# Scales of q and k made during av, seven PSUM banks in turn, two stages' first loads moved forward, a subtraction on POOL

## The chip, the cores and the metric

The kernel runs on one core of a Trainium2 chip. The metric is the device time of one execution in microseconds. Engines are named as in the profile: PE (matmuls), PEld (PE's weight loads), DVE (VectorE), ACT (ScalarE), POOL (GpSimd), SP (which issues the DMAs). The granted clock is the share of TensorE's full clock that the throttle let through.

## The reference

One layer of a decoder trunk on 2048 tokens of width 1024, in float32. Cut to what matters:

```python
h = rmsnorm(x, g_norm)
a_u, a_v, a_gate, q, k, v, b_gate, gate_logits = split(h @ w_in)     # widths 1024, the last 2 x 1024
y_a = spatial_gating(gelu(a_u), gelu(a_v), w_s, b_s, g_v) * silu(a_gate)
y_b = dilated_attention(q, k, v) * silu(b_gate)      # 16 heads of 64; (128,1), (512,4), (2048,16)
g_a, g_b = split(sigmoid(gate_logits))
x = x + (g_a * (y_a @ w_proj_a) + g_b * (y_b @ w_proj_b)) @ w_out
return rmsnorm(x, g_final)
```

`spatial_gating` normalizes gelu(a_v) per token, mixes the 128 positions of each chunk with a masked 128x128 matrix per group of 128 channels, adds b_s and multiplies by gelu(a_u).

## The kernel before

Every float32 product is made of three: each factor is split in a high and a low part in the matmul's own 32-bit format (fp32r), and `mm3` (L97) accumulates hi·hi, hi·lo and lo·hi in PSUM. A weight arrives as `wraw` by one DMA; `ring` puts its two parts into a ring of eight buffers (names `wc`, `wch`, `wcl`; a trailing number in the listings is the buffer's serial number). `split_w` (L82) makes the high part on ACT (L83) and the low part, raw − hi, on DVE or POOL (L86): from av on, POOL does it.

The tokens are worked in two halves of 1024, and each half as two pieces of 512 columns (`X[0]`, `X[1]`, normalized and transposed input, split in two). Stages of a half, with the columns of w_in they use:

- v (5120): `unit_rows` L310, 16 PSUM tiles of 48 matmuls 128x256; the evacuation `ev_v` L347 writes `vst` (two halves in f16) with ACT L356 and DVE L357, and stores it to `v_d`. In the first half each of the four 256-column blocks also gets a scale (`wscale` L223).
- `make_T` L173: differences T1, T2, T3 of the input blocks for a seven-product scheme, each split on ACT (L134) and DVE (L135).
- av (1024): `unit_rows` again, gelu to `avr`, stored to `av_d`; then `make_T4` L189.
- k (4096) and q (3072): `unit_S` L236, four blocks m of 256 columns; each takes one 1 MB load (`wraw2`, two buffers), seven weight combinations W, and seven products of 12 matmuls 128x512, combined with DVE additions into four results. In the first half each block first calls `wscale` twice: a reduce over the columns' absolute values (DVE L227), a maximum over the partitions with that of g_norm (POOL L230, `partition_all_reduce`), and three small DVE operations. The scale keeps q and k within f16; `scales` L365 derives products of them for the attention.
- u and g (0 and 2048): `branch_a` L390 with two `unit_S`; for a group of 128 channels it loads `avg` (gelu(a_v)), the mixing matrix `wst` and `bsb`, and the evacuation of u multiplies by the mixing product `px` (L418).
- First half: b_gate and the first gate (6144, 7168). Between the halves: the second gate, `unit_P` L299.

Then `restore` rebuilds X[1], and the window (L651) runs the attention of 16 heads with filling matmuls between, `seg` by `seg`; `load_qk` and `load_v` fetch its data. The last stage merges and normalizes.

PSUM has eight banks: `pj` two, `pt` three, `ss` two (attention scores), `po` one. Outside the attention `unit_rows` and `unit_P` take `pj` alone, and `unit_S` `pj` and `pt` alternately.

The order on each engine is set when the program is built: a scheduler places instructions by priority and estimated cost, and each engine then runs its own list strictly in that order. A DMA stands in SP's list and waits there for its data and its buffer; what stands behind it waits too.

Of the kernel before, what the change touches and what calls it, by code (L numbers as in the profile page):

```python
# [16 lines left out]
P = 128  # L17
# [10 lines left out]
class Prog:  # L28
    def __init__(self, ctx, tc, io):
        self.ctx, self.tc, self.nc, self.io = ctx, tc, tc.nc, io  # L30
        self.last_pe = None
        self.w_hi, self.w_lo = self.nc.scalar, self.nc.vector
        self.x_lo = self.nc.vector


    def setup(self):
        nc, tc, ctx, io = self.nc, self.tc, self.ctx, self.io
        self.const = c = ctx.enter_context(tc.tile_pool(name="const", bufs=1))
        self.ps = ctx.enter_context(tc.tile_pool(name="ps", bufs=1, space=bass.MemoryType.PSUM))
        dr = ctx.enter_context(tc.tile_pool(name="dr", bufs=1, space=bass.MemoryType.DRAM))  # L40
        self.xp = ctx.enter_context(tc.tile_pool(name="xp", bufs=1))
        self.wk = ctx.enter_context(tc.tile_pool(name="wk", bufs=2))
        self.gn = c.tile([P, KC], F32, name="gn")
        nc.scalar.dma_start(out=self.gn, in_=io["g_norm"])
# [9 lines left out]
        self.sq = c.tile([P, 8], F32, name="sq")  # L54
        self.sk = c.tile([P, 8], F32, name="sk")
# [67 lines left out]
    def pt(self):  # L123
        return self.ps.tile([P, 512], F32, name="pt", tag="pt", bufs=3)


    def alloc_X(self, tt):
        return [[self.xp.tile([P, 512], F32R, name=f"X{tt}_{k}_{p}", tag=f"X{tt}_{k}_{p}") for p in range(2)]
# [44 lines left out]
    def make_T(self, hp, qds):  # L173

        nc = self.nc
        self.TT = {}
        for i in (1, 2, 3):
            self.TT[i] = [[self.tp.tile([P, 512], F32R, name=f"T{i}_{k}_{p}", tag=f"T{i}_{k}_{p}") for p in range(2)]
                          for k in range(4)]
        for k in range(4):  # L180
            b12, b11, b22 = (self.h_chunk(hp, "ht", 4, qds[c], k + r) for c, r in ((1, 0), (0, 0), (1, 4)))
            nc.vector.tensor_sub(b11, b12, b11)
            self.split_X(self.TT[1], k, b11)
            nc.vector.tensor_sub(b12, b22, b12)
            self.split_X(self.TT[3], k, b12)
            nc.vector.tensor_sub(b22, b22, b11)
            self.split_X(self.TT[2], k, b22)

    def make_T4(self, X):  # L189

# [45 lines left out]
    def unit_S(self, X, w, c0, evac, qds, scale=None):  # L236

        nc = self.nc
        B11, B21, B22 = X[0][:4], X[0][4:], X[1][4:]
        for m in range(4):  # L240
            raw = self.wraw(w, c0 + 256 * m)
            a11, a12 = raw[:, 0:4, 0:P], raw[:, 4:8, 0:P]
            a21, a22 = raw[:, 0:4, P:256], raw[:, 4:8, P:256]
            if scale is not None:
                for j in range(2):
                    self.wscale(raw[:, :, j * P:(j + 1) * P], scale(2 * m + j))
            W = [self.ring(a11, 4, P), self.ring(a12, 4, P)]
            s1 = self.wr.tile([P, 4, P], F32, name="s1", tag="s1", bufs=1)
            nc.vector.tensor_add(s1, a21, a22)
# [4 lines left out]
            W += [self.ring(a12, 4, P), self.ring(a22, 4, P)]  # L254

            def prod(i, B):
                ps = (self.pj, self.pt)[i % 2]()
                for _ in self.mm3(ps, lambda a, k: W[i][a][:, k], lambda b, k: B[k][b], range(4)):
                    pass
                return ps  # L260
# [38 lines left out]
    def unit_P(self, X, w, c0, evac, qd):  # L299

        for m in range(4):
            raw = self.wraw(w, c0 + 256 * m)
            for j in range(2):
                W = self.ring(raw[:, :, j * P:(j + 1) * P], KC, P)
                ps = self.pj()
                yield from self.mm3(ps, lambda a, k: W[a][:, k], lambda b, k: X[qd % 2][k][b])
                evac(2 * m + j, qd, ps)
                yield
# [1 line left out]
    def unit_rows(self, X, w, c0, evac, tts, scale=None):  # L310

        W = {}
        for wbs in ((0, 1), (2,), (3,)):
            for tt in tts:
                for wb in wbs:
# [3 lines left out]
                        if scale is not None:  # L319
                            self.wscale(raw, scale(wb))  # L320
                    for np_ in range(2):
                        ps = self.pj()
# [52 lines left out]
    def ev_av(self, vp, hf):  # L375
# [3 lines left out]
        def ev(wb, np_, ps):  # L379
            t = vp.tile([P, 2, 256], F32, name="avr", tag="avr", bufs=2)  # L380
            nc.scalar.activation(t, ps.rearrange("p (c n) -> p c n", c=2), AF.Gelu_apprx_tanh)
            j = vp.tile([P, 256], F16, name="junk", tag="junk", bufs=1)
# [7 lines left out]
    def branch_a(self, ap, hf, X):  # L390
# [41 lines left out]
        qds = (2 * hf, 2 * hf + 1)  # L432
        gu = self.unit_S(X, io["w_in"], 0, ev_u, qds)
        gg = self.unit_S(X, io["w_in"], 2048, ev_g, qds)
        for m in range(4):
            for g in (2 * m, 2 * m + 1):
                gr[g] = group(g)
            yield next(gu)
            yield next(gg)


# [209 lines left out]
    def window(self, at, fill, total_fill):  # L651
# [15 lines left out]
        def run(gen, keep=False):  # L667
# [143 lines left out]
    def run(self):  # L811
# [5 lines left out]
        def drain(g):  # L817
            for _ in g:
                pass
# [4 lines left out]
        with pool("tp", bufs=1) as self.tp, pool("wr", bufs=2) as self.wr, pool("cp", bufs=1) as self.cp:  # L824
            X = [None, None]
            for hf in range(2):
                qds = (2 * hf, 2 * hf + 1)
                with pool(f"hp{hf}", bufs=2) as hp:
# [12 lines left out]
                        X = [X0, self.make_h(hp, 3)]  # L841
                        drain(self.unit_rows(X, win, 5120, rows, (0, 1)))
                    self.make_T(hp, qds)
                    drain(self.unit_rows(X, win, 1024, self.ev_av(hp, hf), (1, 0)))
                self.make_T4(X)
                with pool(f"wq{hf}", bufs=2) as self.wq:
                    for c0, dst, sc in ((4096, self.k_d, self.sk), (3072, self.q_d, self.sq)):
                        drain(self.unit_S(X, win, c0, self.ev_qk(dst, sc), qds,
                                          (lambda nb, sc=sc: sc[:, nb:nb + 1]) if hf == 0 else None))
                if hf == 0:  # L850
                    self.scales()
                with pool(f"ap{hf}", bufs=2) as ap:
                    drain(self.branch_a(ap, hf, X))
# [72 lines left out]
```

## Time and profile before

| | us |
| --- | --- |
| median of 3 runs (lowest, highest) | 2845.96 (2844.33, 2847.51) |
| profiled execution, and its span | 2844.65, 2842.8 |
| PE busy in the span | 2566.0 (90%) |
| DVE, ACT, POOL busy | 1686.8, 1302.7, 808.8 |
| mean granted clock of PE | 0.959 |
| read from HBM, written | 290.00 MB, 109.71 MB |

A row of a view gives a start and a duration in us, the engine, the line of the program, the operation with what it writes and reads, and in brackets how long the engine stood idle before it and what ended that. A row of the waits gives who waited for whom, the sum in us, how often, and the longest.

### The profile page before, as it was taken

How to read it: one execution, taken by the hardware profiler on the slowest of the kernel's cores; microseconds unless marked ns; L12 is line 12 of the kernel's file. 1: busy time of each engine (PE TensorE's matmuls, PEld its weight loads, DVE VectorE, ACT ScalarE, POOL GpSimd, SP SyncE). 2: the span in 40 equal slices, each digit the busy share in tenths (PEclk: the TensorE clock that was granted, in tenths of full speed). 3: DMA queues.
4: the chain of work that ended last, by engine and by line, in shares of the span. 5: the costliest groups of instructions: out<-in, count | busy, mean ns of one | idle time of the engine just before them, and what ended most of it. 6: DMA issues, size and time to landing. Idle time of an engine off the chain costs nothing.

```text
span 2842.8 us, 45723 instructions
## 1 busy us (share of the span) xinstructions
PE 2566.0 (90%) x17024; PEld 2173.3 (76%) x17024; DVE 1686.8 (59%) x3796; ACT 1302.7 (46%) x2455; POOL 808.8 (28%) x606
## 2 busy tenths in 40 slices
PE   4999666999999899999989999988898889899999
PEld 4998445788888899888867777777777767677877
DVE  5504444776532611556746877789888888555443
ACT  4233121334433324343326877778777776332221
POOL 0013223544544112444432221233333343100000
PEclk8999787999999999999999999999999999999999
DMA  7433122434345542343345465666677666765442
GB/s 206 102 84 98 47 60 56 127 101 136 131 137 167 138 94 86 110 117 109 109 130 138 132 175 156 177 181 172 193 226 219 202 186 198 220 203 186 142 145 74
DMA packets 465087, 402.72 MB, mean 142 GB/s; under 512 B 153056, under 2 KB 386912, under 8 KB 464864
## 3 DMA queue, kind: packets, MB, share of 16 engines
q1 hardware_dynamic: 464432, 399.73, 48.6%
q8 instruction: 134, 2.20, 0.3%
q14 instruction: 89, 0.73, 0.1%
q10 hardware_dynamic: 432, 0.07, 0.0%
HBM read 290.00 MB, written 109.71 MB: 141 GB/s over the span
## 4 chain that ended last, share of the span: by engine, by line
PE 58%; DVE 16%; DMA 10%; ACT 7%; issue 5%; POOL 3%; SPq 1%; ACTq 0%; DVEq 0%; POOLq 0%
PE pj L103 42%; PE pt L103 9%; ACT S L556 3%; DVE S L548 3%; POOL wc L86 2%; DVE pl L577 2%; DMA xt<-in_xT 2%; PE pt L573 2%; DMA wraw<-in_w_in 2%; ACT ph L576 1%; PE ss L541 1%; DMA OC<-o_d 1%; DVE OC L631 1%; PE pt L418 1%; PE ss L542 1%
## 5 line engine op out<-in xcount | busy, mean ns | idle before, releaser
L103 PE MATMUL pj<-X,whi 128*128 128x512 f32 x1792 | 598.0, 409 | 14.2 <-POOL whi L85 8.5
L86 POOL TENSOR_TENSOR wc<-wraw,wc 128x512 fp32r<-128x512 f32 x240 | 328.9, 1377 | 403.6 <-ACT wc L83 291.1
L103 PE MATMUL pj<-wch,X 128*128 128x256 f32 x2048 | 383.8, 289 | 39.5 <-DVE vst L357 33.8
L103 PEld LDWEIGHTS pj<-X,whi 128*128 128x128 f32 x1792 | 340.1, 193 | 84.5 <-POOL whi L85 8.9
L103 PE MATMUL pj<-T,wc 128*128 128x512 f32 x1440 | 364.0, 401 | 33.2 <-POOL wc L86 32.2
L103 PE MATMUL pj<-X,wlo 128*128 128x512 f32 x896 | 367.0, 410 | 4.8 <-DVE wlo L86 3.3
L103 PEld LDWEIGHTS pj<-wch,X 128*128 128x128 f32 x2048 | 330.6, 198 | 41.7 <-issue 33.1
L103 PEld LDWEIGHTS pj<-T,wc 128*128 128x128 f32 x1440 | 275.2, 192 | 97.8 <-POOL wc L86 34.3
L103 PE MATMUL pj<-wcl,X 128*128 128x256 f32 x1024 | 295.5, 289 | 4.0 <-DVE wcl L86 4.0
L83 ACT CAST wc<-wraw 128x512 fp32r<-128x512 f32 x240 | 146.0, 619 | 286.8 <-PE pt L103 133.8
L556 ACT ACTIVATE S<-S,ob,iqk 128x128 f32<-128x128 f32 (+1 forms) x512 | 232.0, 526 | 84.4 <-DVE ob L551 83.5
L577 DVE SCALAR_TENSOR_TENSOR pl<-pt,ph 128x512 f16<-128x512 f32 x320 | 206.0, 653 | 94.8 <-ACT ph L576 92.1
L548 DVE CUSTOM_DVE_ANT_0 S<-ss,B 128x256 f32<-128x256 f32 (+1 forms) x768 | 239.5, 358 | 32.6 <-PE ss L542 31.7
L103 PE MATMUL pt<-X,wc 128*128 128x512 f32 x960 | 235.0, 393 | 0.0
L103 PEld LDWEIGHTS pt<-X,wc 128*128 128x128 f32 x960 | 181.8, 190 | 39.2
L103 PEld LDWEIGHTS pj<-X,wlo 128*128 128x128 f32 x896 | 173.9, 194 | 42.7 <-DVE wlo L86 6.3
L103 PEld LDWEIGHTS pj<-wcl,X 128*128 128x128 f32 x1024 | 202.5, 198 | 4.3 <-DVE wcl L86 4.3
L85 POOL TENSOR_SCALAR whi<-wraw 128x1024 fp32r<-128x1024 f32 x64 | 76.7, 1198 | 452.2 <-PE pj L103 423.1
L576 ACT ACTIVATE ph<-pt 128x512 f16<-128x512 f32 x320 | 174.0, 558 | 35.1 <-PE pt L573 27.8
L103 PE MATMUL pj<-WO,X 128*128 128x512 f32 x768 | 181.0, 396 | 1.3 <-ACT X L774 1.1
L573 PE MATMUL pt<-ident,S 128*128 128x128 f32 x1200 | 170.7, 280 | 5.8 <-DVE pl L577 5.7
L103 PE MATMUL pj<-X,wc 128*128 128x512 f32 x480 | 130.5, 423 | 47.8 <-POOL wc L86 44.1
(166 smaller groups left out, 4784.7 us busy)
## 6 DMA issues: line engine op xcount, KB each, us to landing
wraw<-in_w_in SPq DMA_DIRECT2D x64, 1024.0 KB, 5.5
V<-v_d SPq DMA_DIRECT2D x48, 520.0 KB, 4.1
o_d<-ob SPq DMA_DIRECT2D x32, 528.0 KB, 4.2
OC<-o_d SPq DMA_DIRECT2D x32, 528.0 KB, 4.9
xt<-in_xT SPq DMA_DIRECT2D x64, 256.0 KB, 4.5
wraw<-in_w_in SPq DMA_DIRECT2D x32, 512.0 KB, 4.7
wraw<-in_w_proj_a SPq DMA_DIRECT2D x32, 512.0 KB, 4.7
wraw<-in_w_proj_b SPq DMA_DIRECT2D x32, 512.0 KB, 4.6
```

The lines of the kernel that those rows point to most:

```text
L83: nc.scalar.copy(hi, raw)
L85: nc.gpsimd.tensor_scalar(out=hi, in0=raw, scalar1=1.0, scalar2=0.0, op0=ALU.mult, op1=ALU.add)
L86: self.w_lo.tensor_tensor(out=lo, in0=raw, in1=hi.bitcast(F32), op=ALU.subtract)
L103: self.pe = nc.tensor.matmul(out, st(a, k), mv(b, k), start=first and n == 0, stop=last and n == len(todo) - 1)
L418: nc.tensor.matmul(px[:, i * P:(i + 1) * P], av[:, 4 * q + i], w, start=True, stop=True)
L541: nc.tensor.matmul(ps[:, i, :n], q, KH[:, w], start=True, stop=False)
L542: self.pe = nc.tensor.matmul(ps[:, i, :n], q, KL[:, w], start=False, stop=True)
L548: nc.vector.tensor_tensor_reduce(out=S[:, j, :n], in0=ps[:, i, :n], in1=B[:, bo:bo + n], scale=1.0, scalar=-3e38, op0=ALU.add, op1=ALU.max ...
L556: nc.scalar.activation(S[:, i, :rng[i]], S[:, i, :rng[i]], AF.Exp, bias=ob[:, i, 65:66], scale=self.iqk[:, pr:pr + 1])
L573: self.pe = nc.tensor.transpose(px[:, j * P:(j + 1) * P], G["S"][:, i, c * P:(c + 1) * P], self.ident)
L576: nc.scalar.activation(ph[:, :n], px[:, :n], AF.Copy, scale=PSCALE)
L577: nc.vector.scalar_tensor_tensor(out=pl[:, :n], in0=px[:, :n], scalar=PSCALE, in1=ph[:, :n], op0=ALU.mult, op1=ALU.subtract)
```

## The change

- `scales_ahead` (new): in the first half, while av is computed, the eight blocks of k's and q's weights are loaded once more and reduced, 16 columns of maxima; one `partition_all_reduce` over these and g_norm's maximum gives all 16 scales in one tile `skq`. It is a generator, and `run` calls it after every second step of av. `scales` follows. `unit_S` no longer makes scales.
- `bank` (new): outside the attention the PSUM tile comes from `pt`, `ss`, `pj`, `pt`, `ss`, `pt`, `pj` in turn.
- `make_T` subtracts the high part on POOL instead of DVE.
- `branch_a` issues its small loads and its first two groups before k; the other groups are asked for between u and g. It uses the pool of k and q. The scratch tile `junk` of av lies in another pool.
- In the window two of the six times 24/`every` segments of filling work stand ahead of the first `load_qk`, `permuted` and `load_v`.

```diff
+    def bank(self):
+        self.nbank += 1
+        i = self.nbank % 7
+        if i in (0, 3):
+            return self.pj()
+        if i in (1, 4, 6):
+            return self.pt()
+        return self.ps.tile([P, 2, 256], F32, name="ss", tag="ss", bufs=2).rearrange("p a b -> p (a b)")
...
     def make_T(self, hp, qds):
+        self.x_lo = nc.gpsimd
...
+        self.x_lo = nc.vector
...
+    def scales_ahead(self, hp, w, units):
+        nc = self.nc
+        n = 8 * len(units)
+        m = hp.tile([P, n + 1], F32, name="wma", tag="wma", bufs=1)
+        for u, c0 in enumerate(units):
+            for j in range(4):
+                raw = self.wraw(w, c0 + 256 * j)
+                for i in range(2):
+                    c = 8 * u + 2 * j + i
+                    nc.vector.tensor_reduce(out=m[:, c:c + 1], in_=raw[:, :, i * P:(i + 1) * P], axis=AX.XY,
+                                            op=ALU.max, apply_absolute_value=True)
+                yield
+        nc.vector.tensor_copy(m[:, n:n + 1], self.gmax)
+        r = hp.tile([P, n + 1], F32, name="wra", tag="wra", bufs=1)
+        nc.gpsimd.partition_all_reduce(r, m, P, bass_isa.ReduceOp.max)
...
+        nc.vector.reciprocal(out=self.skq, in_=m[:, :n])
+        yield
...
-            if scale is not None:
-                for j in range(2):
-                    self.wscale(raw[:, :, j * P:(j + 1) * P], scale(2 * m + j))
...
-                ps = (self.pj, self.pt)[i % 2]()
+                ps = self.bank()
...                                         # unit_P and unit_rows:
-                ps = self.pj()
+                ps = self.bank()
...                                         # branch_a
+        for g in range(2):
+            gr[g] = group(g)
+        yield
         for m in range(4):
-            for g in (2 * m, 2 * m + 1):
-                gr[g] = group(g)
             yield next(gu)
+            for g in (2 * m + 2, 2 * m + 3):
+                if g < 8:
+                    gr[g] = group(g)
             yield next(gg)
...                                         # window
+        for _ in range(24 // self.every * 2):
+            self.seg(fill)
         raw = {0: self.load_qk(at, 0)}
         for _ in self.permuted(at, raw[0], 2):
             pass
         vt[0, 2] = self.load_v(at, 0, 2)
-        for _ in range(24 // self.every * ahead):
+        for _ in range(24 // self.every * (ahead - 2)):
             self.seg(fill)
...                                         # run
-                    drain(self.unit_rows(X, win, 1024, self.ev_av(hp, hf), (1, 0)))
+                    ahead = self.scales_ahead(hp, win, (4096, 3072)) if hf == 0 else iter(())
+                    for i, _ in enumerate(self.unit_rows(X, win, 1024, self.ev_av(hp, hf), (1, 0))):
+                        if i % 2:
+                            next(ahead, None)
+                    drain(ahead)
+                    if hf == 0:
+                        self.scales()
                 self.make_T4(X)
                 with pool(f"wq{hf}", bufs=2) as self.wq:
+                    branch_a = self.branch_a(self.wq, hf, X)
+                    next(branch_a)
...
```

How it moves instructions, at three places. In the listings a row is an instruction: line, operation, what it writes and reads. POOL at the end of av and the start of k in the first half, before (an `ISA` without operands stands wherever POOL goes over from tensor operations to the all-reduce or back; `wr` is the all-reduce's result):

```order
L230 ISA
L230 ISA wr_2440<-wm_2437 128x2
L230 ISA wr_2448<-wm_2445 128x2
L86 ISA
L86 TENSOR_TENSOR wcl_2168<-wraw2_2165,wch_2167 128x1024
L86 TENSOR_TENSOR wcl_2172<-wraw2_2165,wch_2171 128x1024
L230 ISA
L230 ISA wr_2619<-wm_2616 128x2
L230 ISA wr_2627<-wm_2624 128x2
L86 ISA
L86 TENSOR_TENSOR wc_2453<-wraw2_2435,wc_2453 128x512
```

The same place after (`wra` is the result of the one all-reduce, `wraw2_2502` the first block of k's weights):

```order
L87 TENSOR_TENSOR wcl_2192<-wraw2_2189,wch_2191 128x1024
L87 TENSOR_TENSOR wcl_2196<-wraw2_2189,wch_2195 128x1024
L264 ISA
L264 ISA wra_2428<-wma_1594 128x17
L87 ISA
L87 TENSOR_TENSOR wc_2504<-wraw2_2502,wc_2504 128x512
L87 TENSOR_TENSOR wc_2507<-wraw2_2502,wc_2507 128x512
L87 TENSOR_TENSOR wc_2514<-wraw2_2502,wc_2514 128x512
```

One all-reduce stands between av's last weights and k's first; before, they came two by two between the splits.

DVE at the end of v in the first half, before (`vst` are v's evacuations, and the second name is the PSUM tile they read):

```order
L357 SCALAR_TENSOR_TENSOR vst_1191<-pj_1142,sv_81,vst_1191 128x4x64 x2
L357 SCALAR_TENSOR_TENSOR vst_1250<-pj_1201,sv_81,vst_1250 128x4x64 x2
L357 SCALAR_TENSOR_TENSOR vst_1309<-pj_1260,sv_81,vst_1309 128x4x64 x2
L357 SCALAR_TENSOR_TENSOR vst_1368<-pj_1319,sv_81,vst_1368 128x4x64 x2
L227 TENSOR_REDUCE wm_2437<-wraw2_2435 128x1
L227 TENSOR_REDUCE wm_2445<-wraw2_2435 128x1
```

and after (`wma` collects the maxima; its `wraw2` are the extra loads):

```order
L389 SCALAR_TENSOR_TENSOR vst_1190<-pt_1141,sv_80,vst_1190 128x4x64 x2
L259 TENSOR_REDUCE wma_1594<-wraw2_1719 128x1 x2
L389 SCALAR_TENSOR_TENSOR vst_1249<-pj_1200,sv_80,vst_1249 128x4x64 x2
L259 TENSOR_REDUCE wma_1594<-wraw2_1833 128x1
L389 SCALAR_TENSOR_TENSOR vst_1308<-pt_1259,sv_80,vst_1308 128x4x64
L259 TENSOR_REDUCE wma_1594<-wraw2_1833 128x1
L389 SCALAR_TENSOR_TENSOR vst_1308<-pt_1259,sv_80,vst_1308 128x4x64
L389 SCALAR_TENSOR_TENSOR vst_1367<-ss_1318,sv_80,vst_1367 128x4x64
L259 TENSOR_REDUCE wma_1594<-wraw2_1947 128x1
L389 SCALAR_TENSOR_TENSOR vst_1367<-ss_1318,sv_80,vst_1367 128x4x64
```

Reduces of the extra loads now stand among the evacuations, and these read three kinds of banks instead of `pj` alone.

SP in av of the first half, before (`av_d` are stores of av's results, `avr`; `wraw2_2435` and `wraw2_2614` are k's first two blocks):

```order
L386 DMA av_d0_158<-avr_1819 128x2x256
L209 DMA wraw2_2435<-in_w_in 128x8x256
L386 DMA av_d0_158<-avr_1874 128x2x256
L386 DMA av_d0_158<-avr_1929 128x2x256
L386 DMA av_d0_158<-avr_1994 128x2x256
L209 DMA wraw2_2614<-in_w_in 128x8x256
```

and after (`avr_1827` is av's sixth tile, `wraw2_2309` and `wraw2_2423` the last two extra loads, `wraw2_2502` and `wraw2_2665` k's first two blocks):

```order
L418 DMA av_d0_157<-avr_1827 128x2x256
L222 DMA wraw2_2309<-in_w_in 128x8x256
L418 DMA av_d0_157<-avr_1886 128x2x256
L222 DMA wraw2_2423<-in_w_in 128x8x256
L418 DMA av_d0_157<-avr_1941 128x2x256
L222 DMA wraw2_2502<-in_w_in 128x8x256
L222 DMA wraw2_2665<-in_w_in 128x8x256
```

The extra loads come between the stores; k's first load stands two stores later than before, its second one store earlier.

More of the change, by code (lines that the diff above doesn't have):

```diff
@@ L31, in __init__ @@
         self.last_pe = None
+        self.nbank = 0
         self.w_hi, self.w_lo = self.nc.scalar, self.nc.vector
@@ L53, in setup @@
         nc.vector.tensor_reduce(out=self.gmax, in_=self.gn, axis=AX.X, op=ALU.max, apply_absolute_value=True)
-        self.sq = c.tile([P, 8], F32, name="sq")
-        self.sk = c.tile([P, 8], F32, name="sk")
+        self.skq = c.tile([P, 16], F32, name="skq")
+        self.sk, self.sq = self.skq[:, 0:8], self.skq[:, 8:16]
         self.sv = c.tile([P, 4], F32, name="sv")
@@ L234, in wscale, with unit_S @@
         nc.vector.reciprocal(out=scale, in_=m[:, 0:1])
-    def unit_S(self, X, w, c0, evac, qds, scale=None):
+    def scales_ahead(self, hp, w, units):
[13 more added lines that the diff above has]
+        nc.gpsimd.partition_all_reduce(r, m, P, bass_isa.ReduceOp.max)
+        nc.vector.tensor_scalar(out=m[:, :n], in0=r[:, :n], scalar1=r[:, n:n + 1], scalar2=1.0 / 32.0,
+                                op0=ALU.mult, op1=ALU.mult)
+        nc.vector.tensor_scalar(out=m[:, :n], in0=m[:, :n], scalar1=1e-15, scalar2=None, op0=ALU.max)
+        nc.vector.reciprocal(out=self.skq, in_=m[:, :n])
+        yield
+    def unit_S(self, X, w, c0, evac, qds):
         nc = self.nc
@@ L321, in unit_rows @@
                     for np_ in range(2):
-                        ps = self.pj()
+                        ps = self.bank()
                         for i in range(2):
@@ L381, in ev @@
             nc.scalar.activation(t, ps.rearrange("p (c n) -> p c n", c=2), AF.Gelu_apprx_tanh)
-            j = vp.tile([P, 256], F16, name="junk", tag="junk", bufs=1)
+            j = self.cp.tile([P, 512], F32, name="junk", tag="c", bufs=1)[:, :256]
             for c in range(2):
@@ L843, in run @@
                     self.make_T(hp, qds)
-                    drain(self.unit_rows(X, win, 1024, self.ev_av(hp, hf), (1, 0)))
+                    ahead = self.scales_ahead(hp, win, (4096, 3072)) if hf == 0 else iter(())
[5 more added lines that the diff above has]
+                        self.scales()
                 self.make_T4(X)
                 with pool(f"wq{hf}", bufs=2) as self.wq:
+                    branch_a = self.branch_a(self.wq, hf, X)
+                    next(branch_a)
                     for c0, dst, sc in ((4096, self.k_d, self.sk), (3072, self.q_d, self.sq)):
[L848 to L853, printed above, removed]
+                        drain(self.unit_S(X, win, c0, self.ev_qk(dst, sc), qds))
+                    drain(branch_a)
                 if hf == 0:
```

## The prediction

> **What bounds the kernel now.** I began with the page's busy shares and slices, then cut the span at the stages and asked the waits, POOL's timeline and single tiles for what fills the holes.
>
> ```profile
> span 2842.8 us, 45723 instructions
> core 0: 2842.8 us, clock 0.959
> PE   4999666999999899999989999988898889899999
> PEclk8999787999999999999999999999999999999999
> ```
>
> TensorE is full nearly everywhere; slices 5 to 7 (of 71 us each) are a hole in work and in clock. By stage (columns: stretch, length, busy time and instructions of PE, PEld, DVE, ACT and POOL, granted clock, DMA share, GB/s):
>
> ```profile
> core 0: us, PE busy (x) PEld busy (x) DVE busy (x) ACT busy (x) POOL busy (x), PEclk, DMA share, GB/s
> 58.00:152.00 94.00, 72.06 (x576) 71.19 (x576) 47.04 (x89) 25.43 (x45) 7.53 (x18) 0.91 0.50 106
> 152.00:252.00 100.00, 96.12 (x772) 95.82 (x773) 21.11 (x41) 37.74 (x96) 22.42 (x16) 0.97 0.29 85
> 252.00:517.00 265.00, 185.07 (x692) 145.58 (x691) 126.09 (x185) 59.79 (x103) 86.00 (x71) 0.82 0.24 64
> 517.00:690.00 173.00, 167.99 (x789) 139.18 (x788) 123.78 (x168) 58.15 (x96) 77.88 (x57) 0.99 0.34 105
> 690.00:845.00 155.00, 154.92 (x675) 126.16 (x674) 75.38 (x105) 66.19 (x112) 75.85 (x57) 1.00 0.45 150
> 932.00:1041.00 109.00, 97.75 (x772) 97.14 (x772) 58.31 (x89) 33.95 (x60) 19.86 (x22) 0.94 0.52 117
> 1041.00:1135.00 94.00, 94.00 (x776) 93.59 (x776) 14.10 (x20) 37.41 (x98) 21.61 (x13) 1.00 0.29 88
> 1135.00:1289.00 154.00, 154.00 (x673) 125.91 (x672) 86.75 (x119) 62.19 (x98) 76.93 (x58) 1.00 0.40 110
> 1289.00:1458.00 169.00, 167.18 (x792) 138.59 (x790) 114.99 (x163) 54.73 (x90) 69.68 (x50) 1.00 0.30 92
> 1458.00:2843.00 1385.00, 1258.81 (x9920) 1037.64 (x9920) 966.98 (x2752) 810.61 (x1580) 310.69 (x224) 0.97 0.61 177
> ```
>
> The rows are, of the first half, v (its second part), av, k and q, u and g, bg and ga; of the second half v, av, k and q, u and g; then the window and the end. The case lends its own control: k and q take 265 us in the first half, where scales are computed, and 154 in the second, where they exist, with nearly the same matmuls (692 and 673). What PE waits for before the window:
>
> ```profile
> PE pj L103 <- POOL wc L86: 76.3, 11, 8.6
> PE pj L103 <- DVE vst L357: 33.8, 8, 15.7
> PE pt L418 <- DVE wst L406: 5.7, 2, 3.9
> ```
>
> 76.3 us are weights that POOL splits late, 33.8 are evacuations of v that free a PSUM bank late. Why POOL is late, in its timeline of k's second and third block, and in the waits of k and q:
>
> ```profile
> 304.26 0.37 POOL L230 PARTITION_ALL_REDUCE wr<-wm  x1 [5.94 <-issue]
> 311.60 1.25 POOL L86 TENSOR_TENSOR wc<-wraw,wc 128x512 fp32r<-128x512 f32 x1 [6.97 <-issue]
> ...
> 314.06 4.66 POOL L86 TENSOR_TENSOR wc<-wraw,wc 128x512 fp32r<-128x512 f32 x3
> 326.52 0.37 POOL L230 PARTITION_ALL_REDUCE wr<-wm  x1 [7.80 <-DVE u L266]
> 333.98 2.49 POOL L86 TENSOR_TENSOR wc<-wraw,wc 128x512 fp32r<-128x512 f32 x2 [7.09 <-issue]
> POOL wc L86 <- issue: 78.9, 11, 7.7
> POOL wr L230 <- issue: 46.7, 7, 8.7
> ```
>
> An all-reduce itself takes 0.37 us, but 6 to 8 us pass before it and some 7 us after it in which POOL does nothing: 78.9 + 46.7 = 125.6 us in this stage.
>
> **The change part by part.**
>
> *Scales ahead.* Removed from k and q: 16 all-reduces with those gaps, and 16 reduces. Two prices. Taking only the idle away gives 265 − 185.07 = 79.9. Taking the second half's stage as the result gives 265 − 154 = 111. They differ by the clock: 185.07 us at 0.82 is 151.8 us at full clock, and the second half needed 154.00 at 1.00. The slow clock stood only where PE paused, and the pauses go, so I take 110.5, near the second row; 79.9 stays as the low end. Next in line there would be PE itself, as in the second half, where it is busy 154.00 of 154.
>
> Added: eight 1 MB loads, 16 reduces, one all-reduce over 17 columns.
>
> ```profile
> L227 DVE TENSOR_REDUCE wm<-wraw x20: 1208/1220/2287, 15.6 to 444.7; 128x1 f32<-128x1024 f32 x16, 128x1 f32<-128x2048 f32 x4
> wraw<-in_w_in SPq DMA_DIRECT2D x64, 1024.0 KB, 5.5
> ```
>
> A load lands 5.5 us after its issue and two reduces then take 2 × 1.22 = 2.44 us. By the order, four pairs of reduces stand among v's last evacuations; the last two loads stand on SP behind av_d writes of av's sixth to eighth tile. A tile takes 94.0 × 48 / 776 = 5.81 us. If v ends near 128 (next part), the eighth tile is written near 175, the last load has landed at 180, is reduced at 183, and with 7.8 + 0.4 + 7.1 us of POOL around the all-reduce and 2.5 us for k's first splits the weights stand ready at about 201. av ends at 128 + 93 = 221: 20 us of cover, so this costs 0. Without that cover each us late is a us of time. k's own first load follows these in the queue, two stores later than before, inside the same cover.
>
> *Seven banks.* v and av of the first half need 576 + 772 = 1348 matmuls, at the second half's 94.0 / 776 a time 163.3 us, and take 94 + 100 = 194: at most 30.7 to gain. The evacuations' share:
>
> ```profile
> 73.45 0.55 PE L103 MATMUL pj<-wch,X 128*128 128x256 f32 x1 [15.68 <-DVE vst L357]
> PE pj L103 <- DVE vst L357: 22.5, 5, 15.7
> PE pj L103 <- DVE vst L357: 3.7, 1, 3.7
> PE pj L103 <- DVE vst L357: 11.3, 3, 5.0
> ```
>
> (22.5 in the first half's 57 to 153, 3.7 in its av, 11.3 in the second's 930 to 1042; a wait's columns are its sum, how often, the longest.) The long wait has v's third scale behind it: two tiles fill pj, and nothing moves until one is read. With seven banks PE can be five more tiles, 29 us, ahead, more than the longest wait of 15.7. I take 26 of the 30.7, leaving 5 for a first tile or a weight that is late. Low end: only the short waits go, 22.5 − 15.7 + 3.7 = 10.5. In the second half v takes 109 for 772 matmuls worth 93.5: at most 15.5. All idle there is these waits, 109 − 97.75 = 11.25; low end 11.3 − 5.0 = 6.3; I take 12, for the clock of 0.94 rises too. In the other stages outside the attention PE is busy 154.92 of 155 and the like: banks give 0 there, both ends.
>
> *T's subtraction on POOL.* Twelve a half leave DVE (0.68 us each, 8.2 us) for POOL, which is busy 7.53 of 94 us in v. This speaks against it:
>
> ```profile
> L135 DVE TENSOR_TENSOR T<-xt,T x24: 671/683/2489, 64.5 to 998.9; 128x512 fp32r<-128x512 f32 x24
> 972.54 2.90 DVE L141 SCALAR_TENSOR_TENSOR xt<-xt,gn,rsbc 128x512 f32<-128x512 f32 x1 [0.73 <-DMA xt<-in_xT]
> ...
> 975.97 0.74 DVE L141 SCALAR_TENSOR_TENSOR xt<-xt,gn,rsbc 128x512 f32<-128x512 f32 x1
> 972.49 2.40 POOL L86 TENSOR_TENSOR wcl<-wraw,wch 128x1024 fp32r<-128x1024 f32 x1 [2.79 <-ACT wch L83]
> ```
>
> Beside a POOL subtraction of 2.40 us a DVE operation that takes 0.74 alone took 2.90. Twelve subtractions at 1.25 us can so hold DVE up to 15 us a half, 6.8 more than leaves it. DVE in the first v then carries 47.04 + 4 × 2.44 + 6.8 = 63.6 us of about 70. The seven banks hide that; I cost it at 0, and at the loss of v's gain if they don't (a rival below).
>
> The Trainium skill ("SBUF — State Buffer", section "SBUF: two separate sides") states that a GpSimd operation and a VectorE operation with two SBUF inputs exclude each other for the whole instruction. The trace agrees, 2.90 beside 2.40; with that rule laid on every moved subtraction the sum would be the rival's, without it the main one.
>
> *First pieces asked for sooner.* u and g take 173 and 169 us with PE busy 167.99 and 167.18: 6.8 us idle in all, mostly px waiting for wst (5.7). Loads and scaling of the first two groups now stand ahead of k, some 154 us early. I take 6; ends 3 and 7. In the window the six fill pieces stand earlier in the program, but SP, POOL and PE run in the same order from the attention on, so the gap at its start stays:
>
> ```profile
> 1466.37 1.22 PE L103 MATMUL pj<-X,whi 128*128 128x512 f32 x2 [8.45 <-POOL whi L85]
> ```
>
> I take 0; at best 8.45, if the load comes earlier because what stands ahead of it ends sooner.
>
> *Sum:* 110.5 + 26 + 12 + 6 = 154.5; span 2842.8 − 154.5 = 2688.3. The profiled execution took 2844.65, 1.85 more than its span, and the median of the three runs, 2845.96, is 1.31 above that: 2688.3 + 1.85 + 1.31 = 2691.5. Best ends: 111 + 30.7 + 15.5 + 7 + 8.45 = 172.7, giving 2673.3. Worst ends: 79.9 + 10.5 + 6.3 + 3 = 99.7, giving 2746.3.
>
> **Rivals.**
> (1) DVE becomes the bound of v: reduces that wait for loads and two-input operations that wait for POOL stand in front of evacuations, so the banks fill anyway. For it: 63.6 of 70 us, and the order. Against: 29 us of lead. v and av then gain nothing: 2691.5 + 26 + 12 = 2729.5; half of that 2710.
> (2) The extra loads end late: only two wraw2 buffers, and SP runs in order. If the last two loads had to stand behind av's last tile instead of its eighth, 2 × 5.5 + 2.4 + 15.3 + 2.5 = 31 us would follow av's end: 2722. It decides beyond 20 us of delay.
> (3) Slower: the granted clock falls because PE never rests. PE's 2566 busy us were at a mean of 0.959, 2461 at full clock. The gain is used up when busy time grows by 154.5, from 2535 (31 less in k and q) to 2690: at a mean clock of 0.915. At the 0.82 of the k and q row it would be 3001, that is 2691.5 + 466 = 3157. Against it: bg and ga 155 us, and av with k and q 248 us on end, ran at 1.00; low clocks stand only beside idle PE.
> (4) The edit does nothing: the scheduler would have to have brought the all-reduces back between k's splits; the order shows it has not.
>
> **How the numbers follow.** Main case 2673 to 2705: 0.70. Rival 1: 0.15 (2705 to 2730). Rival 2: 0.11 (2712 to 2746, the case where only the idle goes included). Rival 3: 0.02. Rival 4: 0.01; the rest, 0.01, is a gain past the best end. The range of 2673 to 2726 holds the main case and most of the first two rivals. Of no change, about 0.2% (5.7 us) either way, can be told. Faster 0.97, same 0.01, slower 0.02.
>
> **What would show it.** Right: PE's wait on POOL wc gone from k and q, that stage near 154 us at clock 1.00; one all-reduce of 17 columns, ended before av does; v of the first half near 70 us, of the second near 97; PE matmuls of v into three tile names; the wait on wst gone; 8.45 us still at the window's start. Wrong: a wait on a reduce or on wraw at k's first tile (rival 2), vst waits above 15 us in v beside long DVE operations (rival 1), a clock below 0.95 in a stage without idle PE (rival 3).

## The result and the profile after

The changed kernel takes 2718.43 us in the median of four runs (2715.96 to 2721.57), the kernel before beside it 2845.99; the ratio is 0.9552, 95% interval 0.9536 to 0.9569. The profiled execution took 2720.65 us, its span is 2718.8. Forecast were 2691.5, between 2673 and 2726: the direction and the range held, and of the 154.5 us that the sum promised 124.0 came (2842.8 − 2718.8). The main case, 2673 to 2705 with a chance of 0.70, did not hold: the time lies where rivals 1 and 2 were expected.

The page's first lines, and the waits of PE from 26 to 400 us, v, av, k and q of the first half (sum, how often, longest):

```profile
span 2718.8 us, 45716 instructions
PE   5989999999999999999899899989888889899998
PEclk9989999999999999999899999999999999899999
PE ss L104 <- ACT wch L84: 6.6, 1, 6.6
PE pt L169 <- POOL rs L79: 5.3, 1, 5.3
PE pj L104 <- ACT wch L84: 4.4, 1, 4.4
PE pj L104 <- POOL vst L384: 2.7, 1, 2.7
PE ss L104 <- POOL wcl L87: 2.3, 1, 2.3
```

The hole in slices 5 to 7 is gone, with it the 76.3 us on POOL wc and the 33.8 on vst evacuations. New are waits on ACT's cast of weights (wch), on POOL's subtraction (wcl) and on POOL's memset of vst. By stage:

```profile
core 0: us, PE busy (x) PEld busy (x) DVE busy (x) ACT busy (x) POOL busy (x), PEclk, DMA share, GB/s
26.00:128.00 102.00, 96.01 (x766) 95.48 (x766) 64.75 (x101) 29.41 (x52) 19.20 (x24) 0.97 0.57 128
128.00:241.00 113.00, 96.84 (x771) 95.73 (x770) 39.93 (x54) 43.13 (x106) 27.77 (x21) 0.92 0.60 168
241.00:395.00 154.00, 154.00 (x674) 125.93 (x673) 98.99 (x124) 60.80 (x102) 82.34 (x60) 1.00 0.40 117
395.00:564.00 169.00, 169.00 (x803) 140.71 (x802) 121.06 (x163) 58.44 (x96) 76.22 (x57) 1.00 0.32 99
805.00:907.00 102.00, 96.12 (x774) 95.14 (x773) 49.80 (x73) 31.04 (x55) 36.27 (x30) 0.97 0.52 118
907.00:1001.00 94.00, 93.11 (x774) 92.71 (x774) 16.04 (x24) 37.49 (x96) 19.73 (x13) 1.00 0.35 96
1323.00:2718.00 1395.00, 1264.82 (x9930) 1042.06 (x9928) 967.54 (x2755) 813.31 (x1583) 307.02 (x224) 0.96 0.61 176
```

(v, av, k and q, u and g of the first half; v and av of the second; window and end.) k and q run as in the second half, PE busy all the time at a clock of 1.00. But av, the second row, takes 113 us for work that takes 94 in the second half: it has become the hole.

The table has the length of each stage in us for the profiled executions, between marks at the same numbered matmul of PE in every kernel. In the first half the marks of av, k, u and the gates are the stage's first matmul, and v's is its ninth; in the second half they stand 8 to 16 matmuls (1 to 3 us) ahead of the stage's first, so the wait at the window's start counts to the window. "Before" has both its profiles, the second one taken among the experiments; gates are bg, ga and gb.

| kernel | v 1 | av 1 | k, q 1 | u, g 1 | gates | v 2 | av 2 | k, q 2 | u, g 2 | window, end |
| --- | --- | --- | --- | --- | --- | --- | --- | --- | --- | --- |
| before | 126.8 | 98.8 | 260.7 | 176.1 | 241.0 | 110.5 | 92.2 | 153.5 | 170.8 | 1386.9 |
| before, again | 130.3 | 97.2 | 259.2 | 177.3 | 241.5 | 113.1 | 92.2 | 153.5 | 170.8 | 1389.9 |
| after | 102.5 | 113.0 | 154.3 | 168.8 | 240.4 | 102.5 | 93.6 | 153.5 | 168.8 | 1395.7 |
| ahead_only | 134.8 | 93.6 | 154.3 | 171.1 | 241.2 | 112.9 | 92.2 | 153.5 | 172.5 | 1392.9 |
| banks_only | 102.1 | 101.7 | 261.0 | 178.4 | 240.4 | 98.5 | 97.9 | 153.5 | 172.4 | 1393.7 |
| t_on_dve | 102.3 | 109.0 | 154.3 | 168.8 | 240.4 | 98.5 | 95.7 | 153.5 | 168.8 | 1396.2 |
| late8 | 106.2 | 105.6 | 154.9 | 175.9 | 240.4 | 104.1 | 92.3 | 153.5 | 168.8 | 1395.4 |
| t_vact4 | 104.8 | 106.2 | 154.3 | 169.1 | 240.4 | 97.0 | 93.4 | 153.5 | 169.1 | 1393.4 |
| t_vact4_late8 | 104.2 | 100.4 | 156.3 | 177.8 | 240.4 | 96.5 | 93.0 | 153.5 | 169.1 | 1393.3 |

The kernel before took 2852 to 2854 us in the medians of the four later sets of runs, each on another chip, against 2846 in the first. So the kernels are compared by their ratios to the runs of it beside them, and stages by their lengths.

### The profile page after: what moved, and what is told of

Its sections match the earlier page's. It is cut to its first block, busy times and chain, and to the rows that moved or that the text cites. A ratio compares the mean times of both kernels' runs of the same rounds, so it can differ in the third digit from the quotient of the medians.

```text
span 2718.8 us, 45716 instructions
## 1 busy us (share of the span) xinstructions
PE 2537.4 (93%) x17024; PEld 2155.7 (79%) x17024; DVE 1677.5 (62%) x3712; ACT 1300.4 (48%) x2455; POOL 835.5 (31%) x615
## 4 chain that ended last, share of the span: by engine, by line
PE 64%; DVE 14%; DMA 11%; ACT 6%; issue 3%; SPq 2%; POOL 1%; DVEq 0%; POOLq 0%; ACTq 0%
PE pj L104 29%; PE pt L104 16%; PE ss L104 11%; ACT S L592 3%; DVE S L584 3%; DMA v_d<-vst 2%; DVE pl L613 2%; PE pt L609 2%; DMA xt<-in_xT 2%; DMA OC<-o_d 1%; DVE OC L667 1%; DMA o_d<-ob 1%; SPq L393 1%; PE ss L577 1%; ACT ph L612 1%
## 5 line engine op out<-in xcount | busy, mean ns | idle before, releaser
L613 DVE SCALAR_TENSOR_TENSOR pl<-pt,ph 128x512 f16<-128x512 f32 x320 | 205.6, 652 | 97.2 <-ACT ph L612 94.2
L104 PE MATMUL pt<-T,wc 128*128 128x512 f32 x960 | 235.7, 394 | 0.0
L104 PEld LDWEIGHTS pt<-T,wc 128*128 128x128 f32 x960 | 179.7, 188 | 40.9
L104 PEld LDWEIGHTS pj<-WO,X 128*128 128x128 f32 x768 | 144.2, 188 | 37.3 <-DVE X L813 2.0
L626 PE MATMUL po<-V,ph 128*128 128x65 f16 x1200 | 136.6, 195 | 36.1 <-ACT ob L629 29.3
L104 PE MATMUL pt<-wch,X 128*128 128x256 f32 x864 | 165.2, 289 | 3.4 <-ACT X L145 2.2
L104 PE MATMUL pj<-T,wc 128*128 128x512 f32 x672 | 165.2, 394 | 0.0
L592 ACT ACTIVATE S<-S,OC,iqk 128x256 f32<-128x256 f32 (+1 forms) x256 | 131.5, 584 | 67.0 <-DVE OC L587 66.5
L609 PEld LDWEIGHTS pt<-ident,S 128*128 128x128 f32 x1200 | 142.4, 144 | 26.2 <-DVE pl L613 9.2
L104 PE MATMUL ss<-X,wc 128*128 128x512 f32 x672 | 162.5, 391 | 0.0
## 6 DMA issues: line engine op xcount, KB each, us to landing
wraw<-in_w_in SPq DMA_DIRECT2D x32, 512.0 KB, 4.7
wraw<-in_w_proj_a SPq DMA_DIRECT2D x32, 512.0 KB, 5.3
wraw<-in_w_proj_b SPq DMA_DIRECT2D x32, 512.0 KB, 4.5
```

What stands on the lines that cost most here:

```text
L104: self.pe = nc.tensor.matmul(out, st(a, k), mv(b, k), start=first and n == 0, stop=last and n == len(todo) - 1)
L592: nc.scalar.activation(S[:, i, :rng[i]], S[:, i, :rng[i]], AF.Exp, bias=ob[:, i, 65:66], scale=self.iqk[:, pr:pr + 1])
L609: self.pe = nc.tensor.transpose(px[:, j * P:(j + 1) * P], G["S"][:, i, c * P:(c + 1) * P], self.ident)
L613: nc.vector.scalar_tensor_tensor(out=pl[:, :n], in0=px[:, :n], scalar=PSCALE, in1=ph[:, :n], op0=ALU.mult, op1=ALU.subtract)
L626: nc.tensor.matmul(o, ph[:, sl], V[:, kb, 64:129], start=first, stop=False)
```

## The experiments

**What each part is worth.** Three kernels: T's subtractions back on DVE, and the kernel before with one part alone.

```diff
# t_on_dve (on the changed kernel)
-        self.x_lo = nc.gpsimd          # make_T
# ahead_only (on the kernel before): scales_ahead, skq, no wscale in unit_S; junk in pool cp
# banks_only (on the kernel before): bank() in unit_S, unit_P, unit_rows
```

> The changed kernel with T's subtractions back on DVE; all else kept. In the changed kernel v and av of the first half take 215.5 us together (25.7 to 241.2), 163 to 190 was hoped for. Theory T: the subtractions stand on POOL ahead of the small memset that each evacuation of v needs, so they hold the evacuations. Then v and av of the first half shrink by 8 to 14 us, v and av of the second half by 3 to 6, the time is 2702 to 2708. Theory L: the extra loads and their reduces hold av's own weights and v's evacuations, POOL has no part in it. Then the time is 2714 to 2724.

Measured 0.9518 (0.9497 to 0.9540), against 0.9552: 9.7 us of 2853. v and av of the first half take 211.2 us instead of 215.4, of the second 194.2 instead of 196.1. One profile does not settle this: two kernels below that do not differ from the changed one in these stages (no_groups, no_fill) have 215.7 and 222.3, 196.6 and 197.7. But the pair vst4 and t_vst4, run side by side, gives 0.9541 and 0.9502, 11.1 us, and in its profiles 8.1 us in the first half's v and av and 2.6 in the second's; all six kernels with the subtractions on POOL lie between 0.9540 and 0.9552, the four with them on DVE between 0.9502 and 0.9518. So POOL's subtractions cost about 10 us, at the lower end of theory T's 10 to 16, and L's "no part in it" is wrong; the time itself, 2714.9 beside a kernel before of 2853.2, can't be read against the ranges set from 2846. The 163 us of full use count from v's fifth tile: from there t_on_dve takes 178.5 us, so most of the way has another cause.

> The kernel before with nothing but the scales made ahead (the scratch tile of av moved to another pool so that the maxima find room). Both theories: k and q of the first half near 154 us instead of 260.8. Theory T: v and av of the first half stay at their 225.5 us, time 2736 to 2742. Theory L: they grow by 8 us or more, time above 2747.

Measured 0.9621 (0.9595 to 0.9646). k and q have 154.3 us, with 106.4 gained. v and av take 228.3, against 225.6 and 227.5 in the two profiles of before: the extra loads cost next to nothing where PE waits for evacuations anyway. Theory L's 8 us did not come.

> The kernel before with nothing but the seven banks in turn. If the banks are worth what the prediction said, v and av of the first half lose 26 us and v of the second 12, time 2806 to 2812. If evacuations of v are paced by their stores and buffers whatever the banks, they lose less than half of it: 2828 or more. Theory L expects the first, theory T (POOL's subtractions absent here) too; a time above 2828 speaks against both.

Measured 0.9925 (0.9900 to 0.9950), 14 to 29 us of 2853; the expectation stood at 34 to 40, and the median of 2830.89 lies above the 2828 that was to speak against both theories. v shrinks by 24.7 and 12.0, much as forecast, but av grows by 2.9 and 5.7. The waits of PE in the second half's v and av (905 to 1110) say why:

```profile
PE pt L104 <- POOL wcl L87: 6.6, 2, 4.0
```

PE, now ahead, comes to av before av's weights are split. The banks alone are worth 21.8 and 6.3 us of the first and the second half's v and av, not 30.7 and 15.5.

So of the 21.8 us of the first half the changed kernel keeps 10.1 in its profile: 4.2 go to the subtractions on POOL (215.4 − 211.2; 8.1 in the pair above), and some 7.5 (211.2 − 203.8) to the extra loads, which cost little without the banks. The split is one of single profiles, and these differ by up to 7 us in kernels that do the same here.

**How the extra loads cost it.** DVE of the changed kernel at the start of av (128 on), SP, POOL and ACT beside it:

```profile
136.84 0.48 DVE L389 SCALAR_TENSOR_TENSOR vst<-pt,sv,vst 128x256 f16<-128x256 f32 x1 [0.54 <-ACT vst L388]
145.71 2.35 DVE L259 TENSOR_REDUCE wma<-wraw 128x1 f32<-128x1024 f32 x2 [8.38 <-DMA wraw<-in_w_in]
147.97 0.48 DVE L389 SCALAR_TENSOR_TENSOR vst<-pj,sv,vst 128x256 f16<-128x256 f32 x1
...
153.28 1.22 DVE L259 TENSOR_REDUCE wma<-wraw 128x1 f32<-128x1024 f32 x1 [3.81 <-DMA wraw<-in_w_in]
154.42 0.47 DVE L389 SCALAR_TENSOR_TENSOR vst<-pt,sv,vst 128x256 f16<-128x256 f32 x1
125.53 12.06 SPq L393 DMA_DIRECT2D v_d<-vst  x8
137.82 0.37 SPq L222 DMA_DIRECT2D wraw<-in_w_in  x1
148.08 0.37 SPq L222 DMA_DIRECT2D wraw<-in_w_in  x1
135.45 2.35 POOL L87 TENSOR_TENSOR wcl<-wraw,wch 128x1024 fp32r<-128x1024 f32 x1
154.93 0.48 ACT L388 ACTIVATE vst<-pt,sv 128x256 f16<-128x256 f32 x1 [5.61 <-DVE vst L389]
155.30 1.98 ACT L84 CAST wch<-wraw 128x1024 fp32r<-128x1024 f32 x2
```

v's matmuls ended at 128, but its evacuations are still going on. DVE stands at a reduce until 145.71 for a load that SP issued only at 137.82. That load stood behind eight stores of v, and a `wraw2` buffer came free just then as well, with POOL's subtraction of av's first weights (135.45 + 2.35). The next load follows at 148.08, when these reduces have freed the buffer (145.71 + 2.35), and holds the reduce of 153.28. The evacuations stand on DVE behind the reduces, and ACT's cast of av's second weights, for which PE waits 6.6 us, behind the evacuations. Which link sets the pace? Five kernels cut one or more.

```diff
# late8 (on the changed kernel): extra loads asked for in av's second half
-                        if i % 2:
+                        if 8 <= i:
                             next(ahead, None)
# vst4: four staging tiles of v's evacuation, two of them in u2 and u4 (520 wide); t_vst4: with t_on_dve
+            if self.nv % 4 < 2: t = vp.tile(... tag="vst", bufs=2)
+            else: t = self.cp.tile(... tag=("u2", "u4")[self.nv % 2], bufs=1)
# vact: v's stores on ACT's queue; t_vact4: with t_on_dve and vst4
-                nc.sync.dma_start(out=self.v_d[4 * wb + j]...
+                nc.scalar.dma_start(out=self.v_d[4 * wb + j]...
```

> The changed kernel with the eight extra loads asked for in the second half of av's sixteen steps, one a step, instead of every second step from the start. Theory L: v and av of the first half shrink by 8 to 16 us, as the first extra loads no longer stand ahead of av's second weight block; the reduces end later, but inside av or a few us after; time 2704 to 2712. Theory T: 2714 to 2724.

Measured 0.9551 (0.9524 to 0.9578). av shrinks by 7.4 us, but v grows by 3.7, so that v and av lose 3.7 us and not theory L's 8 to 16; u and g grow by 7.1, and nothing is left.

> The changed kernel with four staging tiles for v's evacuation instead of two (the other two lie in the scratch tiles u2 and u4, free in that stage). Theory S: with banks free the evacuation of v is paced by its two staging tiles, each held until its store has landed, and the stores hold back, in SP's list, the loads of av's weights. Then v and av of the first half go from 215.5 to 200 to 208 us, of the second half from 196.1 to 188 to 192, time 2702 to 2710. Theory L: extra loads and their reduces, which wait in front of evacuations, set the pace: no more than 3 us, 2715 to 2722.

> The same four staging tiles, with T's subtractions on DVE as well. Theory S: both gains, 3 to 4 us from the subtractions and 8 to 15 from the tiles; 2698 to 2707. Theory L: only the subtractions' gain, 2712 to 2716.

Measured 0.9541 (0.9519 to 0.9562) and 0.9502 (0.9483 to 0.9521). With the four tiles v and av of the first half take 219.8 us, within the 215.4 to 222.3 of the kernels without; with the subtractions on DVE as well 211.7, as t_on_dve alone (211.2). Theory S falls: the staging tiles alone do not set the pace.

> The changed kernel with v's stores (v_d) issued by ACT instead of SP, so that loads in SP's list no longer stand behind stores that wait for evacuations. Theory C (a convoy: a reduce on DVE waits for its load, the load stands on SP behind stores of v, the stores wait for an evacuation, and that stands on DVE behind the reduce): the circle is cut; v and av of the first half go from 182 us (25.8 taken as v's start: 69.1 and 113.0) to 165 to 174, of the second from 196 to 188 to 192, ratio to the kernel before 0.948 to 0.951. Rival B: what holds av are the two wraw2 buffers and the reduces alone: first half 178 to 184, ratio 0.954 to 0.957. Rival A: ACT, waiting at the stores for DVE, delays evacuations itself, slower than the changed kernel: above 0.957.

(Its 182 us count from v's fifth tile, at 59.1.) Measured 0.9547 (0.9521 to 0.9573); v and av take 215.3 us, as in the changed kernel, and PE's wait on the cast (from 130 to 241) is still there:

```profile
PE ss L104 <- ACT wch L84: 11.4, 1, 11.4
```

The stores were in the way on SP, but with them gone the two buffers and the reduces hold as much: the load that was issued at 137.82 goes out at 134.03, right behind POOL's subtraction, and the next at 143.23, right behind the reduces that end at 143.21. Theory C falls for rival B. In the second half, where it forecast 188 to 192 us, v and av take 200.8 instead of 196.1.

> v's stores on ACT, T's subtractions on DVE and four staging tiles together. Theory C: v and av of the first half 163 to 170 us, near the 163 of full use; ratio 0.945 to 0.949. Rival B: as with the four tiles and the subtractions alone, 178 us, ratio 0.949 to 0.952.

Measured 0.9508 (0.9492 to 0.9524): 211.0 us for the first half's v and av, rival B again; in the second's, where there are no reduces, 190.3, after 194.2 with the subtractions alone and 193.0 with the four tiles too. That left the reduces themselves.

```diff
# t_vact4_late8 (on t_vact4)
-                        if i % 2:
+                        if 8 <= i:
                             next(ahead, None)
```

> v's stores on ACT, T's subtractions on DVE, four staging tiles, and the extra loads asked for only in the second half of av's steps, so that every reduce stands on DVE behind v's last evacuation. Without the last edit v and av of the first half take 177.8 us and PE waits 9.4 us for the cast of av's second weights. Theory B2 (reduces that wait for their loads stand among v's evacuations on DVE, and the cast of av's weights stands on ACT behind these evacuations): that wait goes, v and av of the first half take 165 to 172 us, ratio to the kernel before 0.946 to 0.949. Rival: the two wraw2 buffers and the loads' own time hold av's weights wherever the reduces stand: 175 to 180 us, ratio 0.950 to 0.952. A second rival: the scales now come after av's end and k waits; the first half's av is short, but more than 5 us of waiting stand at k's first tile.

(Counted from v's fifth tile.) The wait is gone, and v and av take 170.5 us in that count, 204.6 in the table's: theory B2's 165 to 172. The cast of av's second weights starts 14.5 us after av's first matmul, in t_vact4 20.0, in the changed kernel 27.0, in banks_only, without extra loads, 16.1. So the reduces among the evacuations hold av's weights, but not alone. late8 took them from there too, and its cast starts at 20.1, on ACT behind an evacuation that waits for a store of v to free its staging tile:

```profile
151.16 0.47 ACT L388 ACTIVATE vst<-pt,sv 128x256 f16<-128x256 f32 x1 [8.48 <-DMA v_d<-vst]
152.56 1.98 ACT L84 CAST wch<-wraw 128x1024 fp32r<-128x1024 f32 x2
```

Each edit alone leaves the other hold; which of the other three is needed beside late8 was not tried. Yet the ratio is 0.9509 (0.9496 to 0.9522), as without the edit and not B2's 0.946 to 0.949, because k and q now take 156.3 us instead of 154.3 and u and g 177.8 instead of 169.1:

```profile
386.00:564.00 178.00, 170.94 (x802) 140.78 (x801) 151.11 (x173) 59.89 (x103) 82.32 (x60) 1.00 0.31 97
PE pt L104 <- DVE u L297: 4.5, 4, 1.9
389.30 1.77 DVE L280 TENSOR_TENSOR s<-wraw 128x512 f32<-128x512 f32 x1 [0.59 <-POOL wc L87]
391.10 1.65 DVE L281 TENSOR_TENSOR wraw<-wraw 128x512 f32<-128x512 f32 x1
389.24 2.97 POOL L87 TENSOR_TENSOR wc<-wraw,wc 128x512 fp32r<-128x512 f32 x2
```

(The stage, PE's wait in it, and three rows of DVE and POOL.) DVE is busy 151.11 us there; the durations of its 172 instructions in the stage add up to 158.3 us, those of the same 172 in t_vact4 to 130.9. An addition and a subtraction take 1.77 and 1.65 us beside POOL's subtractions. The same two in t_vact4, 0.69 each:

```profile
381.88 0.69 DVE L280 TENSOR_TENSOR s<-wraw 128x512 f32<-128x512 f32 x1 [0.85 <-POOL wc L87]
382.61 0.69 DVE L281 TENSOR_TENSOR wraw<-wraw 128x512 f32<-128x512 f32 x1
```

The order of DVE's list in u and g is the same in both, and so is POOL's; only the phase between them differs. Of the 18 operations of lines 280 and 281 in this stage, 13 take 1.44 to 1.77 us and overlap POOL's subtractions by 0.89 us or more; five take 0.68 or 0.69 and overlap them by 0.31 or less. Why the later scales keep it in the bad phase for most of u and g was not tried.

**Branch_a's first loads, and the window.**

```diff
# no_groups (on the changed kernel): branch_a behind k and q, every group before its u; its pool stays that of k and q
# no_fill (on the changed kernel): all six times 24/every segments behind load_v, as before
```

> The changed kernel with branch_a as it was: its loads and first groups behind k and q. By the prediction's term 6 us come back: u and g of the first half from 168.8 to 172 to 175 us, of the second from 168.8 to 171, time 2722 to 2726. A rival: the loads hide anyway now that POOL no longer stalls, and the time stays 2716 to 2721.

Measured 0.9540 (0.9521 to 0.9559); u and g take 168.8 and 168.8 us, exactly as with the edit. But this kernel does not bring the late loads back. It restores the order of the program and leaves branch_a in the pool of k and q, and SP still issues its first loads at k's start. The first of them in the first half, in the kernel before (u starts at 512.0), ahead_only (408.4), no_groups (396.4) and the changed kernel (395.5), and what PE waits for in u and g of ahead_only:

```profile
523.18 0.35 SPq L393 DMA_DIRECT2D mk<-in_causal  x1
416.30 0.35 SPq L415 DMA_DIRECT2D mk<-in_causal  x1
245.84 0.40 SPq L425 DMA_DIRECT2D mk<-in_causal  x1
245.03 0.40 SPq L425 DMA_DIRECT2D mk<-in_causal  x1
PE pt L440 <- DVE wst L428: 2.1, 1, 2.1
```

In the three kernels where branch_a has a pool of its own (before, ahead_only, banks_only) these loads come behind q's last stores, 8 to 13 us after u's start, and PE waits at the mixing product: 3.9, 2.1 and 6.9 us in the first half, 1.7 to 1.9 in the second. In no_groups and the changed kernel it does not wait. So the rival, that the loads hide anyway, was not tested, and where the loads stand and PE waits speaks for the prediction's reading. With the scales alone u and g of the first half lose 5.0 us of the 7.3, with the banks alone none, and neither alone shortens the second's. A kernel with both and the old pool was not run, so the share of the early loads stays an estimate: 2.3 us (171.1 − 168.8) in the first half and 2.0 in the second.

> The changed kernel with the window's start as it was. By the prediction's term of 0 nothing changes: 2716 to 2721, the wait of 8 to 10 us at the window's start stays. A rival, since the window of the changed kernel took 1395.7 us in its profile and the one before 1386.9: the earlier fill pieces cost 9 us, and without them the time is 2708 to 2711.

> The kernel before, unchanged, profiled once more. Its first profile has the window (from the end of u and g to the end of the span) at 1386.9 us, while all kernels since, with the same instruction lists there, took 1393 to 1400. If the window's length differs from run to run, it is 1390 to 1400 here; if something in the changed parts lengthens it, 1386 to 1388 again.

no_fill measured 0.9547 (0.9525 to 0.9570), the same as with the edit, with a window of 1400.2 us. The kernel before has 1389.9 in its second profile, just short of the 1390 to 1400 that were named for a varying window. Both kernels in which nothing of the window was edited (ahead_only, banks_only) have 1392.9 and 1393.7, so the edit is not what makes it longer. What does, within 1387 to 1400, stays open.

## Why the prediction came out as it did

- *Scales: 110.5 forecast, 106.4 measured.* The mechanism was right throughout: all of the idle went, the clock went from 0.82 to 1.00, and the second half's stage was the right control. The 4 us are a boundary: the row 252 to 517 contained 5 us of u (which began at 512.0); from start to start the two stages are 260.7 and 154.3 (106.4).
- *The cover of the extra loads.* k's weights were to stand ready at 201, with 20 us to spare:

```profile
L264 POOL PARTITION_ALL_REDUCE wra<-wma x1: 422/422/422, 210.5 to 210.5; - x1
220.60 2.54 POOL L87 TENSOR_TENSOR wc<-wraw,wc 128x512 fp32r<-128x512 f32 x2 [9.68 <-ACT avr L413]
```

  They stood ready at 223, and k began at 241.2: late by 22, and still 18 ahead, since av was late as well. Rival 2 looked at the right loads and at the wrong victim: it was av's own second weight block that waited.
- *Seven banks in the first half: 26 forecast, 10.1 measured.* The step that failed is "the seven banks hide that". They do in v, which ended at 128.3 (128 was forecast). But the lead is not free time: evacuations of v that PE has left behind are done during av, on the engines that prepare av's weights. The full-use floor of 163 us for v and av was no measure, since nothing in the rows of before showed av's weights ready that early; banks_only shows 21.8 and not 30.7 from the banks. The 5 us left for "a first tile or a weight that is late" were too few: PE waits 6.6, 4.4 and 2.3 us for av's weights. The reduces in front of evacuations, priced at 9.8 us of DVE's busy time, cost about 7.5 by waiting for loads in an ordered list. Rival 1 named these reduces, but not what they hold: its sign, vst waits above 15 us in v, did not come (the longest in this half is 2.7), v gained 24.3 us, and av lost 14.2.
- *T's subtractions on POOL: 0 forecast, about 10 us measured by the ratios,* in both halves together, 4.2 and 1.9 in one pair of profiles, 8.1 and 2.6 in the other. The row of 2.90 us had shown the price, and "the seven banks hide that" waved it away. Rival 1's price, 19 to 38 us (2710 to 2729.5), holds the loss in these stages, 15.9 + 5.4 = 21.3 us, and the time lies in its band, which had a chance of 0.15. It lies in rival 2's band as well, by luck: k waited for nothing.
- *Second half: 12 forecast, 6.6 measured.* v lost 8.0, av got 1.4 back; with the subtractions on DVE 8.5.
- *First pieces: 6 forecast for u and g, 9.3 measured.* 5.0 of it come with the scales alone, which the sum did not count in this stage; the other 4.3 stand where the loads are early, within the ends of 3 and 7, but no run isolates them. The reading of the wait on wst, a load asked for too late, fits every trace. To bring the load forward the pool of k and q was enough, without the new order of the program.
- *Window edit: 0 forecast, 0 measured,* and the wait at its start stays (8.45 us before):

```profile
PE pj L104 <- POOL whi L86: 10.3, 1, 10.3
```

  The stage itself is 8.8 us longer than in the first profile of before, and 5.8 than in the second. The sum took one profile's window as fixed, and that is 9 of the 30.5 us by which it missed.
- *Rivals 3 and 4.* The clock rose, from 0.959 to 0.976 in the mean; no stage without idle PE had less than 1.00.

t_vst4, t_vact4 and t_vact4_late8 have the lowest ratios, 0.9502 to 0.9509, with intervals below that of the changed kernel (from 0.9536 on). What pays in them is T's subtractions on DVE; the staging tiles, the stores on ACT and the later loads add nothing that these ratios can tell.

## What to carry to other kernels

When a buffer is added so that an engine can run ahead, price the next stage's inputs too: the lead is spent where the work left behind shares a queue or an engine with the preparation of what comes next. An instruction that waits for a transfer, put on an in-order engine ahead of work on which others wait, costs its wait and not its busy time: here 8.38 us before two reduces that take 2.35. An experiment that takes an edit back has to move in the trace what the edit moved: no_groups put the program's order back, and the loads stayed where they were. And a stage's gain should be measured from start to start of its first instruction, with a second profile of the kernel before to tell how far a stage moves by itself.

## What the runs showed of the hardware

DVE's time for the same 172 instructions depended on its phase against POOL by 27 us in a stage of 170 (158.3 and 130.9 us in sum), enough to make PE wait 7.1 us. The Trainium skill ("SBUF — State Buffer", section "SBUF: two separate sides") says that a DVE operation with two inputs in SBUF and a POOL operation that reads SBUF exclude each other on a shared port pair for a whole instruction. The rows of 1.77 us beside 2.97 us on POOL agree, and that the phase persists over most of the stage's eight weight blocks is what the case adds. The window's length differed by 13 us between profiles (1386.9 in the kernel before, 1400.2 in no_fill), and v with av of the first half by 7 (215.4 in the changed kernel, 222.3 in no_fill), with the program unchanged there.
